# A float32 decoder trunk: 18 instead of 14 channel blocks of three FFN halves in Strassen pairs, with the products in another order

## The chip, the cores and the metric

The kernel runs on one core of one Trainium2 chip. The metric is the device time of one execution in microseconds, lower is better. The engines are named as the profile names them: PE (TensorE, matmul), PEld (its weight loads), DVE (VectorE), ACT (ScalarE), POOL (GpSimd) and SP (SyncE, which issues most DMAs).

## The reference, cut to what matters

Two layers work on x, 512 tokens by 1024 channels, all in float32. Each layer is an FFN half, a token mixer and a second FFN half, so there are four FFN halves. The change touches three of them.

```python
def swiglu(h, wg, wu, wd):
    return (jax.nn.silu(h @ wg) * (h @ wu)) @ wd

for li in range(DEPTH):                    # two layers
    h = rmsnorm(x, g[0])
    x = x + 0.5 * rmsnorm(swiglu(h, ffn_wg[li, 0], ffn_wu[li, 0], ffn_wd[li, 0]), g[1])
    ...                                    # the mixer of the layer
    h = rmsnorm(x, g[4])
    x = x + 0.5 * rmsnorm(swiglu(h, ffn_wg[li, 1], ffn_wu[li, 1], ffn_wd[li, 1]), g[5])
```

wg and wu are 1024 x 2816 and wd is 2816 x 1024. The 2816 hidden channels are 22 blocks of 128.

## The kernel before, in words

**Numbers.** Every float32 operand of a matmul is split into two float32r parts, hi and lo. A product takes three matmuls: hi by hi, hi by lo and lo by hi. The split of a weight block (128 x 1024) is an ACT copy to `whi` (L87) and a DVE subtraction to `wlo` (L88). h stands transposed in `self.hi` and `self.lo` (hT_hi, hT_lo in the trace): 8 chunks of 128 channels, 512 tokens each.

**Stages.** `PLAN` (L43) runs FFN (0,0), mixer 0, FFN (0,1), FFN (1,0), mixer 1, FFN (1,1). An FFN half (`ffn`, L691) has a lead of three blocks f = 0 to 2 (`lead`), then the rest of the 22 blocks, then the tail (`tail`, L549), which multiplies the 22 results g by wd into four accumulators `acc`, one for each 128 tokens, and runs the norms. FFN (0,0) uses plain blocks only and is not touched.

**A plain block** (L732 to L743) takes two weight blocks, wg and wu of one f. Each is 8 chunks by 3 matmuls of 512 columns (`chmajor`), 48 matmuls in all; then a Silu on ACT and a multiplication on DVE give g[f].

**A Strassen pair** (`paired_body`, L822) does two f at once, four weight blocks. Tokens are cut in halves and input channels in halves (quarters A11, A12, A21, A22 of h), output channels f and f+1 in columns of B11, B12, B21, B22. In the form of Winograd, seven products take the place of eight; each product is 2 (wg, wu) by 4 chunks by 3 = 24 matmuls of 256 columns. The left factors A11, A12, A22 are views of h; S1 to S4 are sums of quarters that `left_factors` (L759) makes once for each FFN half, on DVE through PSUM, and splits into SBUF tiles. S3 = A11 - A21 and S4 get small tiles of tag "g". The right factors T1 to T4 are sums of weight blocks, made on DVE in `prep_to` (L109, L112, L117, L120) ahead of their split. The seven products of a pair are, in the order of before: A11 into bank a, S2 into b, S1 into c, A12 added onto a, S3 added onto b, A22 into d, S4 added onto c. Between them ACT copies a (L858), and DVE makes the sums in the SBUF tile R: R1 = b + R0 (L861), R0 = b + R0 (L868), R2 = c + R0 (L869), R0 = d + R0 (L872), R1 = c + R1 (L876). So L869 has to read c after S3 and before S4 is added onto it. Silu and multiplication follow for each quarter (L865 to L879).

**Where the blocks stand.** f = 0 to 3 are plain (three of them the lead), f = 4 to 17 are seven pairs, and f = 18 to 21 are plain again, after the pairs. A21 is the one quarter of h that no product of a pair reads; the plain blocks read all of h.

**Buffers.** PSUM has four tiles of two banks (`bank2`), for the pairs a, b, c and d. Eight buffers each hold `whi` and `wlo` (`NW`): a split can run seven weight items ahead of PE. Four `raw` buffers (`NRAW`) take the loads of 512 KB; two buffers of tag "T" take T1 and T2/T4; 26 of tag "g" (`NG`) hold g, the parts of S3 and S4, and the splits of g for the tail.

**Order.** Inside `paired` and `tail` the order of PE is the one written. The order of the instructions on DVE, ACT and SP is chosen by the framework's planner, from its own estimate of times; each engine then takes its instructions in that order.

Of the kernel before, what the change touches and what calls it, by code (L numbers as in the profile page):

```python
# [33 lines left out]
AHEAD = {"mix0": 4, "mix1": 2}  # L34
LEAD = 3
NG = NF + 4
PAIRS = {("ffn", 0, 1): 7, ("ffn", 1, 0): 7, ("ffn", 1, 1): 7}
PLAIN = 4
SIDE = 6
SIDE_AT = 8  # L40
WARM = 20
# [8 lines left out]
class WeightStream:  # L50
# [18 lines left out]

    def add_pairs(self, fours):  # L70
        for four in fours:
            self.items += [(k, len(self.blocks)) for k in ("B11", "T2", "T1", "B21", "T3", "T4", "B22")]
            self.blocks += four

    def load_to(self, n):
# [15 lines left out]
    def prep_to(self, n):  # L91
        V, raw = self.nc.vector, self.raw
        while self.ready < min(n, len(self.items)):
            i = self.ready
            kind, r = self.items[i]
            self.ready += 1

            def t(k):
                raw[r, k] = self.t_pool.tile([P, 1024], F32, tag="T", name=f"T{k}_{r}", bufs=2)
                return raw[r, k]  # L100

            if kind == "block":
                self.load_to(r + 1)
                self.split(i, raw.pop(r))
                self.load_to(r + 1 + NRAW)
                continue
            self.load_to(r + {"B11": 2, "T2": 3, "T1": 3}.get(kind, 4))
            if kind == "B11":
                V.tensor_sub(t(1), raw[r + 1], raw[r])  # L109
                self.split(i, raw.pop(r))  # L110
            elif kind == "T2":
                V.tensor_sub(t(2), raw[r + 2], raw[r, 1])  # L112
                self.split(i, raw[r, 2])
            elif kind == "T1":
                self.split(i, raw.pop((r, 1)))
            elif kind == "B21":
                V.tensor_sub(raw[r, 2], raw[r + 3], raw[r, 2])  # L117
                self.split(i, raw.pop(r + 3))
            elif kind == "T3":
                V.tensor_sub(raw[r + 1], raw[r + 2], raw[r + 1])  # L120
                self.split(i, raw.pop(r + 1))
            elif kind == "T4":
                self.split(i, raw.pop((r, 2)))
            else:
                self.split(i, raw.pop(r + 2))
            self.load_to(r + {"B21": 5, "T3": 6, "T4": 6, "B22": 7}.get(kind, 4))

    def get(self, i, ahead=None):
        self.prep_to(i + 1 if ahead is None else ahead)
# [261 lines left out]
class Trunk:  # L391
# [24 lines left out]
    def phase_blocks(self, ph, ws):  # L416
        a = self.a
        if ph[0] == "ffn":
            _, li, s = ph
            n = PAIRS.get(ph, 0)  # L420

            def plain(fs):
                for f in fs:
                    ws.add([a["wg"][li, s, f], a["wu"][li, s, f]])

            plain(range(PLAIN))
            if n:
                ws.add_pairs([[a["gu"][li, s, e, k] for k in (0, 1, 3, 2)] for e in range(n)])
            plain(range(PLAIN + 2 * n, NF))
            return ws.add([a["wd"][li, s, f] for f in range(NF)])  # L430
        if ph[0] == "mix0":
            r = [a["even_in"][b, t] for b in (2, 1, 0) for t in range(4)]
            r += [a["even_out"][k] for k in range(4, 8)] + [a["glu"][t] for t in range(2)]
            return ws.add(r + [a["even_out"][k] for k in range(4)])
        if ph[0] == "mix1":
            q, f, cm, tm = 4, 8, a["odd_cm"], a["odd_tm"]
            r = [cm[i + h] for h in range(4) for i in (f, q)]
            r += [tm[b, t] for b in (1, 0, 2) for t in range(4)]
            return ws.add(r + [a["odd_out"][k] for k in range(KC)])
        raise ValueError(ph)  # L440
# [250 lines left out]
    def ffn(self, ph, nxt):  # L691
# [4 lines left out]
        with self.tc.tile_pool(name=f"ffn{nm}", bufs=1, reuse_waits="tile") as fp:  # L696
            self.room = fp
            g = {}
            side = None
            if ph == ("ffn", 0, 0):  # L700
                self.s5 = S5Tables(self, fp)
                side = self.s5.build()

            def gtile(dt, what):
                return fp.tile([P, S], dt, tag="g", name=f"{what}{nm}", bufs=NG)

            def act(f, pg):
                g[f] = gtile(F32, f"g{f}")
                nc.scalar.activation(g[f], pg[:, 0, :], AF.Silu)
                self.gated = nc.vector.tensor_mul(g[f], g[f], pg[:, 1, :]).ins  # L710

            split = {}

            def split_to(n):
                for e in range(n):
                    if e in g:
                        gh, gl = gtile(F32R, f"gh{e}"), gtile(F32R, f"gl{e}")
                        gv = g.pop(e)
                        nc.scalar.copy(gh, gv)
                        nc.vector.tensor_sub(gl, gv, gh.bitcast(F32))  # L720
                        split[e] = gh, gl

            n = PAIRS.get(ph, 0)
            ws.t_pool = fp
            self.lead(first, nm, act)
            if n:
                left = self.left_factors(gtile, fp, nm)
            if ph == PLAN[0]:
                self.masks(fp)
                with self.tc.issue_after(self.gated):  # L730
                    self.lower_bound()
            for f in (*range(LEAD, PLAIN), *range(PLAIN + 2 * n, NF)):  # L732
                if n and f == PLAIN + 2 * n:
                    self.paired(first + 2 * PLAIN, n, left, g, gtile, fp, nm)
                    left = None
                pg = self.bank2(f"gu{nm}_{f}")
                for j in range(2):
                    i = first + 2 * f + j + (3 * n if f >= PLAIN else 0)
                    last = self.chmajor(pg[:, j], ws.get(i, i + NW - 1))
                    ws.drop(i)  # L740
                if f == NF - 2:
                    split_to(2)
                act(f, pg)  # L743
                if side is not None:
                    self.s5.last, self.s5.chunk = last, f
                    for _ in range(NF if f == SIDE_AT + 7 else SIDE):
                        next(side, None)

            def stat(f):
                split_to(f + 2)  # L750
                return split.pop(f)

            self.g_post = self.load_gain(li, 2 * 2 * s + 1, "g_post")
            if nxt is not None:
                self.g_pre = self.load_gain(*self.pre_index(nxt), "g_pre")
            self.tail(NF, stat, first + 2 * NF + 3 * n, ph, nxt)
            self.room = None

    def left_factors(self, gtile, fp, nm):  # L759

# [47 lines left out]
        left["S4"] = done(s4, small("S4"))  # L810
        s3 = sums("S3")
        V.tensor_sub(s3, w11, w21)
        left["S3"] = done(s3, small("S3"))
        for name, q in (("A11", a11), ("A12", a12), ("A22", a22)):
            left[name] = tuple(views(v) for v in q)
        return left

    def paired(self, first, n, left, g, gtile, fp, nm):
        with self.tc.manual_schedule(engines={mybir.EngineType.PE}):
            self.paired_body(first, n, left, g, gtile, fp, nm)  # L820

    def paired_body(self, first, n, left, g, gtile, fp, nm):  # L822

# [20 lines left out]
        def new(name):  # L846
            return self.bank2(name)[:, :, 0:256]
# [1 line left out]
        state = {}  # L849

        for e in range(n):
            f = PLAIN + 2 * e
            R = fp.tile([P, 3, 512], F32, tag="R", name=f"R{nm}_{e}", bufs=2)
            R = R.rearrange("p a (m t) -> p a m t", m=2)
            g[f], g[f + 1] = gtile(F32, f"g{f}"), gtile(F32, f"g{f + 1}")
# [1 line left out]
            product(a, "A11", True, False)  # L857
            nc.scalar.copy(R[:, 0], a)  # L858
            b = new(f"sb{nm}_{e}")
            product(b, "S2", True, False)  # L860
            V.tensor_add(R[:, 1], b, R[:, 0])  # L861
            c = new(f"sc{nm}_{e}")
            product(c, "S1", True, False)
            product(a, "A12", False, True)
            nc.scalar.activation(g[f][:, 0:256], a[:, 0], AF.Silu)  # L865
            V.tensor_mul(g[f][:, 0:256], g[f][:, 0:256], a[:, 1])
            product(b, "S3", False, True)
            V.tensor_add(R[:, 0], b, R[:, 0])  # L868
            V.tensor_add(R[:, 2], c, R[:, 0])  # L869
            d = new(f"sd{nm}_{e}")  # L870
            product(d, "A22", True, True)
            V.tensor_add(R[:, 0], d, R[:, 0])  # L872
            nc.scalar.activation(g[f][:, 256:512], R[:, 0, 0], AF.Silu)
            V.tensor_mul(g[f][:, 256:512], g[f][:, 256:512], R[:, 0, 1])
            product(c, "S4", False, True)
# [643 lines left out]
def paired_blocks(wg, wu):  # L1519


    n = max(PAIRS.values())
    w = np.stack([wg, wu])[..., PLAIN * P:(PLAIN + 2 * n) * P].reshape(2, 2, 2, 2, 4, P, n, 2, P)
    return np.ascontiguousarray(w.transpose(1, 2, 6, 3, 7, 5, 0, 4, 8)).reshape(2, 2, n, 4, P, 1024)


# [37 lines left out]
```

## Time and profile before

| | us |
|---|---|
| median of 3 runs | 1933.02 (1931.67 to 1933.94) |
| the profiled execution | 1933.73 |
| its span, first to last instruction | 1932.0 |
| busy PE / DVE / ACT / POOL | 1854.2 / 1152.9 / 679.4 / 300.5 |

The busy time of PE overstates its work, since the ends of matmuls are modelled and overlap. The pace of PE is read from the starts of successive matmuls, and its gaps from the start of the last matmul of one product to the first of the next.

### The profile page before, as it was taken

The numbers are of one execution on the slowest core, as the hardware profiler recorded it, in microseconds if no ns is written. First come the engines' busy times: TensorE is split into PE (matmuls) and PEld (weight loads), VectorE is DVE, ScalarE is ACT, GpSimd is POOL, SyncE is SP. The second block draws the span as 40 slices with busy tenths as digits, with TensorE's granted clock in tenths as the row PEclk, the third lists the DMA queues.
The fourth block names the chain that finished last, engine by engine and source line by source line (L and its number), as shares of the span: only waits on it lengthen the run. The fifth ranks groups of instructions, "written<-read, shape, count | busy, mean of one in ns | idle before, by whom it ended". The sixth has DMA issues, their size and how long they took to land.

```text
span 1932.0 us, 26666 instructions
## 1 busy us (share of the span) xinstructions
PE 1854.2 (96%) x10760; PEld 1625.4 (84%) x10760; DVE 1152.9 (60%) x1739; ACT 679.4 (35%) x919; POOL 300.5 (16%) x530
## 2 busy tenths in 40 slices
PE   8999999989898999999999999999999989999998
PEld 8888888869787999888799998888988779998886
DVE  5756434285958887433698773428634598874333
ACT  4223323132243444332334442313434334443320
POOL 6037750032402000000100000003222020000000
PEclk8999999989999999999999999999999999999999
DMA  6434432243312333533213343332311123334311
GB/s 223 127 123 150 126 106 97 77 164 119 99 35 86 89 109 99 155 96 96 68 55 100 97 153 109 91 95 80 109 45 60 41 86 89 108 99 142 98 55 44
DMA packets 59595, 193.25 MB, mean 100 GB/s; under 512 B 6576, under 2 KB 13744, under 8 KB 59472
## 3 DMA queue, kind: packets, MB, share of 16 engines
q1 hardware_dynamic: 50544, 182.48, 30.4%
q10 hardware_dynamic: 7680, 5.24, 0.8%
q0 software_dynamic: 1248, 3.84, 0.6%
q8 instruction: 84, 1.38, 0.3%
q14 instruction: 39, 0.32, 0.0%
HBM read 182.10 MB, written 9.44 MB: 99 GB/s over the span
## 4 chain that ended last, share of the span: by engine, by line
PE 81%; DVE 12%; DMA 3%; ACT 2%; issue 2%; DVEq 0%; SPq 0%; ACTq 0%
PE accffn L647 16%; PE accffn L649 8%; PE guffn L547 7%; PE guffn L545 7%; PE guffn L546 7%; DMA raw<-in_gu_dram 3%; PE accmix L647 2%; PE scffn L840 2%; PE scffn L841 2%; DVE wlo L88 2%; PE scffn L842 2%; PE leadffn L546 2%; PE leadffn L545 2%; PE leadffn L547 2%; PE saffn L841 1%
## 5 line engine op out<-in xcount | busy, mean ns | idle before, releaser
L87 ACT CAST whi<-raw 128x1024 fp32r<-128x1024 f32 x314 | 328.7, 1050 | 701.2 <-PE accffn L649 183.5
L88 DVE TENSOR_TENSOR wlo<-raw,whi 128x1024 fp32r<-128x1024 f32 x270 | 332.3, 1231 | 406.8 <-ACT whi L87 406.4
L88 POOL TENSOR_TENSOR wlo<-raw,whi 128x1024 fp32r<-128x1024 f32 x44 | 106.8, 2453 | 1004.8 <-ACT whi L87 991.8
L545 PE MATMUL guffn<-hT_hi,whi 128*128 128x512 f32 x544 | 216.3, 398 | 0.0
L547 PE MATMUL guffn<-hT_hi,wlo 128*128 128x512 f32 x544 | 215.5, 396 | 0.0
L546 PE MATMUL guffn<-hT_lo,whi 128*128 128x512 f32 x544 | 213.8, 393 | 0.0
L547 PEld LDWEIGHTS guffn<-hT_hi,wlo 128*128 128x128 f32 x544 | 102.1, 188 | 25.0
L546 PEld LDWEIGHTS guffn<-hT_lo,whi 128*128 128x128 f32 x544 | 102.2, 188 | 24.5
L545 PEld LDWEIGHTS guffn<-hT_hi,whi 128*128 128x128 f32 x544 | 102.2, 188 | 23.5
L546 PE MATMUL leadffn<-hT_lo,whi 128*128 128x256 f32 x352 | 100.7, 287 | 0.0
L547 PE MATMUL leadffn<-hT_hi,wlo 128*128 128x256 f32 x352 | 100.7, 287 | 0.0
L545 PE MATMUL leadffn<-hT_hi,whi 128*128 128x256 f32 x352 | 100.5, 288 | 0.0
L842 PE MATMUL saffn<-hT_hi,wlo 128*128 128x256 f32 x336 | 94.9, 282 | 0.0
L841 PE MATMUL saffn<-hT_lo,whi 128*128 128x256 f32 x336 | 94.8, 282 | 0.0
L840 PE MATMUL saffn<-hT_hi,whi 128*128 128x256 f32 x336 | 94.4, 281 | 0.0
L87 ACT CAST whi<-T 128x1024 fp32r<-128x1024 f32 x63 | 66.3, 1052 | 72.8 <-issue 26.3
L88 DVE TENSOR_TENSOR wlo<-T,whi 128x1024 fp32r<-128x1024 f32 x63 | 76.8, 1218 | 9.2 <-ACT whi L87 9.2
L546 PEld LDWEIGHTS leadffn<-hT_lo,whi 128*128 128x128 f32 x352 | 68.1, 194 | 0.0
L545 PEld LDWEIGHTS leadffn<-hT_hi,whi 128*128 128x128 f32 x352 | 68.1, 195 | 0.0
L547 PEld LDWEIGHTS leadffn<-hT_hi,wlo 128*128 128x128 f32 x352 | 68.0, 193 | 0.0
L840 PEld LDWEIGHTS saffn<-hT_hi,whi 128*128 128x128 f32 x336 | 63.6, 189 | 0.1
L841 PEld LDWEIGHTS saffn<-hT_lo,whi 128*128 128x128 f32 x336 | 63.2, 188 | 0.1
(783 smaller groups left out, 4694.4 us busy)
## 6 DMA issues: line engine op xcount, KB each, us to landing
raw<-in_wd_dram SPq DMA_DIRECT2D x88, 512.0 KB, 3.6
raw<-in_gu_dram SPq DMA_DIRECT2D x84, 512.0 KB, 3.7
raw<-in_wg_dram SPq DMA_DIRECT2D x46, 512.0 KB, 3.7
raw<-in_wu_dram SPq DMA_DIRECT2D x46, 512.0 KB, 3.7
raw<-in_even_in_dram SPq DMA_DIRECT2D x12, 512.0 KB, 3.7
raw<-in_odd_tm_dram SPq DMA_DIRECT2D x12, 512.0 KB, 3.8
raw<-in_even_out_dram SPq DMA_DIRECT2D x8, 512.0 KB, 4.6
raw<-in_odd_cm_dram SPq DMA_DIRECT2D x8, 512.0 KB, 3.7
```

Of the source, the lines that this page charges most:

```text
L87: nc.scalar.copy(hi, raw)
L88: (nc.gpsimd if i in self.early else nc.vector).tensor_sub(lo, raw, hi.bitcast(F32))
L545: nc.tensor.matmul(out, sh, mh, start=start, stop=False)
L546: nc.tensor.matmul(out, sh, ml, start=False, stop=False)
L547: return nc.tensor.matmul(out, sl, mh, start=False, stop=stop).ins
L647: nc.tensor.matmul(acc[:, h, :], gh, w[:, h * 512:(h + 1) * 512], start=first, stop=False)
L649: nc.tensor.matmul(acc[:, h, :], gl, wh[:, h * 512:(h + 1) * 512], start=False, stop=stop)
L840: nc.tensor.matmul(o, wh[:, q], ah[k], start=start and k == 0, stop=False, skip_group_check=True)
L841: nc.tensor.matmul(o, wh[:, q], al[k], start=False, stop=False, skip_group_check=True)
L842: nc.tensor.matmul(o, wl[:, q], ah[k], start=False, stop=stop and k == 3, skip_group_check=True)
```

## The change

1. `PAIRS` goes from 7 to 9 for FFN (0,1), (1,0) and (1,1). f = 0 to 3 stay plain, f = 4 to 21 are nine pairs, and no plain block is left behind the pairs.
2. The factor S3 is no longer split into small tiles in `left_factors`. Its sum stays in PSUM until the plain block f = 3 is done; `rest()` then splits it into the place of the quarter A21 of hi and lo. So the tiles of tag "g" suffice for 22 g.
3. The order of the products is A11 into a, S2 into b, S1 into c, S3 into d, A12 onto a, A22 into b, S4 onto c. R0 is made as d + R1, and R2 = c + R0 follows it; both stand two products ahead of S4 instead of one. b is written anew by A22 instead of being added onto by S3.
4. In the weight stream T3 stands ahead of B21, with the loads moved to match.
5. The splits of g[0] and g[1] for the tail take the two buffers of tag "T" and are made in the last pair; before, they took tiles of tag "g" in the plain block f = 20.

```diff
-PAIRS = {("ffn", 0, 1): 7, ("ffn", 1, 0): 7, ("ffn", 1, 1): 7}
-PLAIN = 4
+PAIRS = {("ffn", 0, 1): 9, ("ffn", 1, 0): 9, ("ffn", 1, 1): 9}
...
-            self.items += [(k, len(self.blocks)) for k in ("B11", "T2", "T1", "B21", "T3", "T4", "B22")]
+            self.items += [(k, len(self.blocks)) for k in ("B11", "T2", "T1", "T3", "B21", "T4", "B22")]
...
-            self.load_to(r + {"B11": 2, "T2": 3, "T1": 3}.get(kind, 4))
+            self.load_to(r + {"B11": 2, "T2": 3, "T1": 3, "T3": 3}.get(kind, 4))
...
-            self.load_to(r + {"B21": 5, "T3": 6, "T4": 6, "B22": 7}.get(kind, 4))
+            self.load_to(r + {"T3": 5, "B21": 6, "T4": 6, "B22": 7}.get(kind, 4))
...
-            plain(range(PLAIN))
+            plain(range(NF - 2 * n))
             if n:
                 ws.add_pairs([[a["gu"][li, s, e, k] for k in (0, 1, 3, 2)] for e in range(n)])
-            plain(range(PLAIN + 2 * n, NF))
...
-                        gh, gl = gtile(F32R, f"gh{e}"), gtile(F32R, f"gl{e}")
+                        if ph in PAIRS and e < 2:
+                            t = fp.tile([P, 2, S], F32R, tag="T", name=f"gs{nm}_{e}", bufs=2)
+                            gh, gl = t[:, 0], t[:, 1]
+                        else:
+                            gh, gl = gtile(F32R, f"gh{e}"), gtile(F32R, f"gl{e}")
...
-            for f in (*range(LEAD, PLAIN), *range(PLAIN + 2 * n, NF)):
-                if n and f == PLAIN + 2 * n:
-                    self.paired(first + 2 * PLAIN, n, left, g, gtile, fp, nm)
-                    left = None
+            for f in range(LEAD, NF - 2 * n):
...
+            if n:
+                self.paired(first + 2 * (NF - 2 * n), n, left(), g, split_to, gtile, fp, nm)
...
         s3 = sums("S3")
         V.tensor_sub(s3, w11, w21)
-        left["S3"] = done(s3, small("S3"))
...
+        def rest():
+            left["S3"] = done(s3, [[v] for v in a21])
+            return left
+
+        return rest
...
             b = new(f"sb{nm}_{e}")
-            product(b, "S2", True, False)
+            product(b, "S2", True, True)
             V.tensor_add(R[:, 1], b, R[:, 0])
             c = new(f"sc{nm}_{e}")
             product(c, "S1", True, False)
+            d = new(f"sd{nm}_{e}")
+            product(d, "S3", True, True)
+            V.tensor_add(R[:, 0], d, R[:, 1])
+            V.tensor_add(R[:, 2], c, R[:, 0])
             product(a, "A12", False, True)
             nc.scalar.activation(g[f][:, 0:256], a[:, 0], AF.Silu)
             V.tensor_mul(g[f][:, 0:256], g[f][:, 0:256], a[:, 1])
-            product(b, "S3", False, True)
+            if e == n - 1:
+                split_to(2)
+            product(b, "A22", True, True)
             V.tensor_add(R[:, 0], b, R[:, 0])
-            V.tensor_add(R[:, 2], c, R[:, 0])
-            d = new(f"sd{nm}_{e}")
-            product(d, "A22", True, True)
-            V.tensor_add(R[:, 0], d, R[:, 0])
```

## Rows read from the trace of the kernel before

**Rows 1.** The page: span, chain that ended last, a costly group (busy, mean ns).

```profile
span 1932.0 us, 26666 instructions
...
PE 81%; DVE 12%; DMA 3%; ACT 2%; issue 2%; DVEq 0%; SPq 0%; ACTq 0%
...
L87 ACT CAST whi<-raw 128x1024 fp32r<-128x1024 f32 x314 | 328.7, 1050 | 701.2 <-PE accffn L649 183.5
```

**Rows 2.** Waits: who waited for whom, us in total, times, longest us.

```profile
PEld scffn L840 <- DVE Rffn L869: 19.9, 15, 1.8
PE scffn L840 <- DVE Rffn L869: 16.8, 15, 1.6
```

**Rows 3.** Windows: length, busy (count) PE, PEld, DVE, ACT, POOL; clock, DMA share, GB/s.

```profile
685.52:706.73 21.21, 20.24 (x171) 20.03 (x169) 17.16 (x20) 9.06 (x11) 0.00 (x0) 1.00 0.35 100
749.38:769.36 19.98, 19.98 (x171) 19.98 (x170) 15.41 (x18) 9.39 (x12) 0.00 (x0) 1.00 0.34 106
642.77:834.13 191.36, 186.09 (x1369) 176.29 (x1368) 127.51 (x142) 75.18 (x93) 0.00 (x0) 1.00 0.38 116
1015.25:1206.46 191.21, 186.10 (x1370) 176.30 (x1368) 127.98 (x142) 75.20 (x93) 0.00 (x0) 1.00 0.38 116
1608.01:1800.42 192.41, 186.02 (x1370) 176.22 (x1368) 127.47 (x142) 75.19 (x93) 0.00 (x0) 1.00 0.37 112
```

**Rows 4.** Timeline (start, us), PE: first matmuls of plain block f=21 and tail.

```profile
822.94 0.39 PE L545 MATMUL guffn<-hT_hi,whi 128*128 128x512 f32 x1
...
834.13 0.40 PE L647 MATMUL accffn<-whi,gh0ffn 128*128 128x512 f32 x1
```

**Rows 5.** Timeline, PE: first matmuls of A11, S3, A22, S4, next A11, third pair.

```profile
685.52 0.28 PE L840 MATMUL saffn<-hT_hi,whi 128*128 128x256 f32 x1
...
697.02 0.28 PE L840 MATMUL sbffn<-S3h0ffn,whi 128*128 128x256 f32 x1
...
699.82 0.28 PE L840 MATMUL sdffn<-hT_hi,whi 128*128 128x256 f32 x1
...
703.83 0.38 PE L840 MATMUL scffn<-S4h0ffn,whi 128*128 128x256 f32 x1 [0.97 <-DVE Rffn L869]
...
706.73 0.28 PE L840 MATMUL saffn<-hT_hi,whi 128*128 128x256 f32 x1
```

**Rows 6.** Timeline, PE: first matmuls of A11, S3, A22, S4, next A11, sixth pair.

```profile
749.38 0.28 PE L840 MATMUL saffn<-hT_hi,whi 128*128 128x256 f32 x1
...
760.88 0.28 PE L840 MATMUL sbffn<-S3h0ffn,whi 128*128 128x256 f32 x1
...
763.68 0.28 PE L840 MATMUL sdffn<-hT_hi,whi 128*128 128x256 f32 x1
...
766.56 0.28 PE L840 MATMUL scffn<-S4h0ffn,whi 128*128 128x256 f32 x1
...
769.36 0.28 PE L840 MATMUL saffn<-hT_hi,whi 128*128 128x256 f32 x1
```

**Rows 7.** Timeline, DVE, third pair, after its product S3.

```profile
700.21 1.23 DVE L109 TENSOR_TENSOR T<-raw,raw 128x1024 f32<-128x1024 f32 x1 [0.41 <-DMA raw<-in_gu_dram]
701.35 0.68 DVE L868 TENSOR_TENSOR Rffn<-sbffn,Rffn 128x512 f32<-128x512 f32 x1
701.95 1.22 DVE L88 TENSOR_TENSOR wlo<-T,whi 128x1024 fp32r<-128x1024 f32 x1
703.09 0.68 DVE L869 TENSOR_TENSOR Rffn<-scffn,Rffn 128x512 f32<-128x512 f32 x1
703.69 1.22 DVE L120 TENSOR_TENSOR raw<-raw,raw 128x1024 f32<-128x1024 f32 x1
704.82 1.22 DVE L112 TENSOR_TENSOR T<-raw,T 128x1024 f32<-128x1024 f32 x1
705.95 0.68 DVE L872 TENSOR_TENSOR Rffn<-sdffn,Rffn 128x512 f32<-128x512 f32 x1
```

**Rows 8.** Timeline, SP: load of a norm gain, queued among the weight loads.

```profile
775.30 0.39 SPq L488 DMA_DIRECT2D g_post<-in_norm_g_dram  x1
```

More of the change, by code (lines that the diff above doesn't have):

```diff
@@ L115, in prep_to @@
                 self.split(i, raw.pop((r, 1)))
+            elif kind == "T3":
+                V.tensor_sub(raw[r + 1], raw[r + 2], raw[r + 1])
+                self.split(i, raw.pop(r + 1))
             elif kind == "B21":
@@ L118, in prep_to @@
                 self.split(i, raw.pop(r + 3))
-            elif kind == "T3":
-                V.tensor_sub(raw[r + 1], raw[r + 2], raw[r + 1])
-                self.split(i, raw.pop(r + 1))
             elif kind == "T4":
@@ L731, in ffn @@
                     self.lower_bound()
-            for f in (*range(LEAD, PLAIN), *range(PLAIN + 2 * n, NF)):
-                if n and f == PLAIN + 2 * n:
-                    self.paired(first + 2 * PLAIN, n, left, g, gtile, fp, nm)
-                    left = None
+            for f in range(LEAD, NF - 2 * n):
                 pg = self.bank2(f"gu{nm}_{f}")
                 for j in range(2):
-                    i = first + 2 * f + j + (3 * n if f >= PLAIN else 0)
+                    i = first + 2 * f + j
                     last = self.chmajor(pg[:, j], ws.get(i, i + NW - 1))
@@ L812, in left_factors, with paired, paired_body @@
         V.tensor_sub(s3, w11, w21)
-        left["S3"] = done(s3, small("S3"))
         for name, q in (("A11", a11), ("A12", a12), ("A22", a22)):
             left[name] = tuple(views(v) for v in q)
-        return left
-    def paired(self, first, n, left, g, gtile, fp, nm):
+        def rest():
+            left["S3"] = done(s3, [[v] for v in a21])
+            return left
+        return rest
+    def paired(self, first, n, left, g, split_to, gtile, fp, nm):
         with self.tc.manual_schedule(engines={mybir.EngineType.PE}):
-            self.paired_body(first, n, left, g, gtile, fp, nm)
-    def paired_body(self, first, n, left, g, gtile, fp, nm):
+            self.paired_body(first, n, left, g, split_to, gtile, fp, nm)
+    def paired_body(self, first, n, left, g, split_to, gtile, fp, nm):
         nc, ws = self.nc, self.ws
@@ L851, in paired_body @@
         for e in range(n):
-            f = PLAIN + 2 * e
+            f = NF - 2 * n + 2 * e
             R = fp.tile([P, 3, 512], F32, tag="R", name=f"R{nm}_{e}", bufs=2)
@@ L1522, in paired_blocks @@
     n = max(PAIRS.values())
-    w = np.stack([wg, wu])[..., PLAIN * P:(PLAIN + 2 * n) * P].reshape(2, 2, 2, 2, 4, P, n, 2, P)
+    w = np.stack([wg, wu])[..., -2 * n * P:].reshape(2, 2, 2, 2, 4, P, n, 2, P)
     return np.ascontiguousarray(w.transpose(1, 2, 6, 3, 7, 5, 0, 4, 8)).reshape(2, 2, n, 4, P, 1024)
```

## The prediction

> **What bounds the kernel now.** I read the page first. PE carries 81% of the chain that ended last and DVE 12%; the span is 1932.0 us, and the execution took 1933.73, so 1.73 lie around the span [rows 1]. A chain that is PE for four fifths says that matmul time comes off the end one for one, and the DVE share says that PE also waits for DVE somewhere. So I asked next who waited for whom. The first matmul of S4 waits for L869, the sum R2 = c + R0, 15 times, on the weight-load side and on the matmul side alike; the two rows are the same 15 waits seen by both halves of the engine and are not to be added [rows 2]. There are 21 pairs (7 in each of 3 FFN halves), so 15 of them stall.
>
> Then the prices, from starts of matmuls, since their ends are modelled. The clock in the stages concerned is 1.00 of 2.4 GHz throughout, so the clock plays no part [rows 3]. A plain block runs from 822.94 to 834.13: 11.19 us [rows 4]. A pair without the stall, the sixth, runs from 749.38 to 769.36: 19.98 us. In it the four products ahead of S3 take 11.50 (2.88 each, rounded), S3 2.80, A22 2.88, S4 2.80 [rows 6]. So products on the small tiles of S3 and S4 are 0.08 us shorter than those on views of h. A stalled pair, the third, takes 21.21: A22 starts at 699.82 and S4 only at 703.83, 4.01 later where 2.88 would do [rows 5]. Two plain blocks cost 22.38, so a stalled pair wins only 1.17 over them and a free one 2.40.
>
> The stall itself is read on DVE. S3 ends about 699.82, where A22 starts. DVE is then idle at the head of its queue for a DMA, makes L109 for a later pair (700.21), then L868 (701.35), then a weight split (701.95), and only then L869 (703.09 to 703.77), 0.06 ahead of S4 [rows 5, 7]. The lag from the end of S3 to the end of L869 is 3.95 us, and one product, 2.88, is all the cover it has. The longest of the 15 waits is 1.8 [rows 2], a lag near 4.7.
>
> **The sum over the three stages.** From the first pair to the tail the stages take 191.36, 191.21 and 192.41, 574.98 together [rows 3]. As a test of the prices: 7 x 19.98 + 4 x 11.19 = 184.62 each, 553.86 together; the other 21.1 us are the stalls, 1.4 in each of 15. After the change each stage is nine pairs.
> - *The two blocks swapped for a pair*, six times: 22.38 - 19.98 = 2.40 each, 14.4 us gained.
> - *The order of the products.* R0 and R2 now follow S3 with A12 and A22 between them and S4: cover 5.75 instead of 2.88. A lag of 3.95 to 4.7 fits with 1.0 us to spare, so I take the whole 21.1 as gained. The other end is nothing gained (below).
> - *S3 in the place of A21.* Its matmuls then read a view of h like A11's: 2.88 instead of 2.80, 0.08 x 27 = 2.2 us lost. The end on the other side is 0, if the short pace is not tied to the tile; I take the loss, since both products on small tiles in rows 6 have 2.80 and all on views have 2.88.
>
> A pair becomes 20.06, a stage 180.5, the three 541.6: 33.4 us less.
>
> **What I cost at nothing, and its cover.**
> - *The late split of S3.* It can start only when f = 3 has ended, where the first pair begins: one ACT copy of 128x1024 (1.05 us [rows 1]) and one DVE subtraction (about 1.2, as the 128x1024 rows of [rows 7]). S3 is needed 3 products later, at 8.63; what may queue ahead on DVE (two or three operations of 1.13) still fits. Its PSUM tile stays taken until then; A11 and S2 have other tiles and S1 starts 5.75 in. If A11 had to wait for it, it would be 2.3 us, 6.8 for three stages: the other end. Below nothing it can't go, as f = 3 has no PE gap to give back.
> - *The tail's start.* The third accumulator may take c's bank: L876 has to read it after the last S4. Two accumulators of six matmuls of 0.233 (11.19 / 48 [rows 4]) go first, 2.80 us; L876 takes 0.7 and at most one split of 1.2 ahead of it. Cover enough; with a second split 0.5 us, 1.6 in three tails. Before, plain blocks stood here.
> - *g[0], g[1] split in the last pair*: two short ACT copies and DVE subtractions, where no sums for a next pair are left to make. The tag-T buffers that they wait for were read one pair earlier.
> - *More weight sums.* Six more pairs mean 24 more sums and 18 more splits on DVE. DVE is busy 17.16 in a stalled pair, ACT 9.06 [rows 3]: 86% and 45% of 20.06.
> - *Loads.* Four of 512 KB in 20.06 instead of 21.21; the DMA share of 0.35 [rows 3] becomes 0.37. T3 ahead of B21 frees one raw buffer as early as B21 did. The two norm gains wait on SP for S2's last product [rows 8], now late in the last pair; behind them stand loads of wd blocks needed at least three products later.
>
> For these edges I add 0.8 us in all, an estimate between 0 and the 8.4 of the ends, and nearer to 0: the stage sum above, of pairs, plain blocks and stalls, leaves no room for a gap at either edge now [rows 3].
>
> Profiled execution: 1933.73 - 33.4 + 0.8 = 1901.1. That execution lies 0.7 above the median of the runs, so the median forecast is 1900.4, taken as 1900.5.
>
> **The rivals.**
> *DVE is the clock.* The free pairs are the last two of each stage, for which no further sums are made: DVE is busy 15.41 there against 17.16 [rows 3]. So no row shows a pair with the full load at 20 us. If the stall is only where DVE's lateness comes out, it comes out elsewhere and 21 pairs (7 of 9, as 5 of 7 now) keep 1.4 us: 29.4 lost again, 1930. The Trainium skill speaks for this one: "Trainium Kernel Development and Optimization", Best Practices, warns that tiling speeds up the matmuls but not the evacuation of PSUM, and a Strassen pair trades just so. Against it: 17.16 is 2.9 below 20.06, and the idle time of DVE in the row is spent waiting on others. Chance 0.10, of which 0.04 within 0.2%.
>
> *The wait moves to b, lightly.* b is now read last by the sum after A22, and the next pair's S2 writes it anew: cover S4 and A11, 5.68. Before, that sum (L872) read d, which was not needed for six products. Its lag is now 706.63 - 702.70 = 3.9 [rows 5, 7], behind L120 and L112. Each further 128x1024 operation that the planner puts ahead costs 1.13. With two more the lag is 6.2: 0.5 in 21 pairs, 11 us, 1911. Chance 0.10.
>
> *The same, heavily: slower than before.* Three more operations and one wait of 0.41 for a load at the head of DVE's queue [rows 7] make a lag of 7.7, 2.05 in each of 21 pairs, 43 us: 1943. It decides from 1.77 a pair, a lag near 7.45. For it speaks that the planner does place sums for later pairs ahead of urgent ones (L109 ahead of L868); against it, that the number of operations between is the same as before and their places are released by the same products. Chance 0.08.
>
> **How the numbers follow.** The forecast, 1900.5, has 0.72. Its own bounds: 1897.5 without the loss on S3, 1906 with most of the edges at their dear end; other stages are planned anew too, and equal stages differ by 1.2 us already [rows 3], so 1895 to 1906. To hold 8 in 10 the range takes in the light wait on b: 1895 to 1913. A measurement of this kernel tells 0.2%, 3.9 us, from no change. Faster: 0.72 + 0.10 + 0.06 = 0.88; same 0.04; slower 0.08.
>
> **What would show it.** Right: no row of waits in which S4's first matmul waits for the R2 sum; pairs 20.06 apart from the second to the eighth; S3 at 2.88; stages near 180.5 and the tail starting with no gap. Wrong: a first matmul of A11 or S2 waiting for DVE (b or a not yet read); A11 of the first pair waiting for the split of S3; DVE busy to the brim in the pairs; pairs that stay at 21.

## The result, and the profile after

| | us |
|---|---|
| before, median of 4 runs beside it | 1933.48 (1931.67 to 1935.71) |
| after, median of 4 runs | 1900.69 (1899.38 to 1902.05) |
| ratio | 0.983, 95% interval 0.9813 to 0.9847 |
| the profiled execution of after | 1899.38 |

The forecast was 1900.5, from 1895 to 1913. The page of after, span and chain, against [rows 1]:

```profile
span 1897.6 us, 27701 instructions
...
PE 89%; DVE 8%; issue 1%; ACT 1%; DMA 0%; DVEq 0%; SPq 0%; ACTq 0%
```

PE's share of the chain went from 81% to 89%, DVE's from 12% to 8%. The windows, against [rows 3] (columns as there): the third pair, then the three stages from the first pair to the tail.

```profile
681.12:701.19 20.07, 20.07 (x171) 20.07 (x170) 17.19 (x20) 8.98 (x11) 0.00 (x0) 1.00 0.35 105
640.99:821.58 180.59, 180.59 (x1513) 180.59 (x1512) 149.51 (x166) 81.81 (x101) 0.00 (x0) 1.00 0.40 120
1002.72:1183.32 180.60, 180.60 (x1514) 180.59 (x1512) 149.31 (x166) 81.82 (x101) 0.00 (x0) 1.00 0.39 120
1585.39:1765.99 180.60, 180.60 (x1513) 180.60 (x1512) 149.21 (x166) 81.86 (x101) 0.00 (x0) 1.00 0.38 117
```

In each of the four, PE is busy for the whole length. The stages add up to 541.79 against 574.98, so 33.2 us of the gain lie in them; the span fell by 34.4. The waits of after have no row for S4's first matmul. In its place stands a row of the opposite sense, DVE waiting for the product S3 (us in total, times, longest us):

```profile
DVE Rffn L873 <- PE sdffn L849: 15.4, 24, 0.7
```

The timeline of PE in after (start, us): S3, A12, S4 and the next A11 in the third pair, then the last matmul of the ninth pair and the first of the tail.

```profile
689.75 0.28 PE L847 MATMUL sdffn<-hT_hi,whi 128*128 128x256 f32 x1
...
692.63 0.28 PE L847 MATMUL saffn<-hT_hi,whi 128*128 128x256 f32 x1
...
698.39 0.28 PE L847 MATMUL scffn<-S4h0ffn,whi 128*128 128x256 f32 x1
...
701.19 0.28 PE L847 MATMUL saffn<-hT_hi,whi 128*128 128x256 f32 x1
...
821.47 0.28 PE L849 MATMUL scffn<-S4h1ffn,wlo 128*128 128x256 f32 x1
821.58 0.64 PE L645 MATMUL accffn<-whi,gsffn 128*128 128x512 f32 x2
```

S3 takes 2.88 (689.75 to 692.63), S4 2.80 (698.39 to 701.19), and the tail follows the last pair at the pace of the matmuls. The timeline of DVE in the same pair, which answers to [rows 7]:

```profile
692.83 0.69 DVE L873 TENSOR_TENSOR Rffn<-sdffn,Rffn 128x512 f32<-128x512 f32 x1 [0.63 <-PE sdffn L849]
693.55 0.69 DVE L874 TENSOR_TENSOR Rffn<-scffn,Rffn 128x512 f32<-128x512 f32 x1
694.16 1.22 DVE L87 TENSOR_TENSOR wlo<-raw,whi 128x1024 fp32r<-128x1024 f32 x1
696.02 1.23 DVE L108 TENSOR_TENSOR T<-raw,raw 128x1024 f32<-128x1024 f32 x1 [0.64 <-DMA raw<-in_gu_dram]
697.16 1.22 DVE L87 TENSOR_TENSOR wlo<-T,whi 128x1024 fp32r<-128x1024 f32 x1
698.29 0.42 DVE L877 TENSOR_TENSOR g8ffn<-g8ffn,saffn 128x256 f32<-128x256 f32 x1
698.63 0.68 DVE L881 TENSOR_TENSOR Rffn<-sbffn,Rffn 128x512 f32<-128x512 f32 x1
```

R0 (L873) and R2 (L874) now follow S3 at once: R2 ends at 694.24, 1.6 after S3's end at 692.63, and 4.15 before S4. The sum T1 (L108), the one that waits for a load at the head of DVE's queue, stood ahead of them in [rows 7] (there L109); here it stands behind. Its place in the pair hardly moved: 14.69 us after the pair's start before (685.52 to 700.21), 14.90 after (681.12 to 696.02). S3's end moved, from 14.30 into the pair to 11.51. Between the first pair and the tail, T1 is made five times in a stage of seven pairs and seven times in a stage of nine, each time two pairs ahead of its use (an experiment below shows it). The 15 stalls of [rows 2] are one for each of these T1; the last two pairs of a stage, which make none, run free.

### The profile page after: what moved, and what is told of

It is laid out like the page before. It is cut to its first block, busy times and chain, and to the rows that moved or that the text cites. A ratio compares the mean times of both kernels' runs of the same rounds, so it can differ in the third digit from the quotient of the medians.

```text
span 1897.6 us, 27701 instructions
## 1 busy us (share of the span) xinstructions
PE 1837.0 (97%) x11192; PEld 1638.0 (86%) x11192; DVE 1220.2 (64%) x1814; ACT 701.1 (37%) x946; POOL 302.0 (16%) x530
## 4 chain that ended last, share of the span: by engine, by line
PE 89%; DVE 8%; issue 1%; ACT 1%; DMA 0%; DVEq 0%; SPq 0%; ACTq 0%
PE accffn L645 16%; PE accffn L647 8%; PE guffn L543 4%; PE guffn L545 4%; PE guffn L544 4%; PE saffn L848 3%; PE sbffn L848 3%; PE sbffn L847 3%; PE sbffn L849 3%; PE saffn L849 3%; PE saffn L847 3%; PE scffn L848 3%; PE scffn L849 3%; PE scffn L847 3%; PE accmix L645 2%; PE leadffn L544 2%
## 5 line engine op out<-in xcount | busy, mean ns | idle before, releaser
L543 PE MATMUL guffn<-hT_hi,whi 128*128 128x512 f32 x352 | 141.0, 401 | 0.0
L545 PE MATMUL guffn<-hT_hi,wlo 128*128 128x512 f32 x352 | 138.8, 394 | 0.0
L544 PE MATMUL guffn<-hT_lo,whi 128*128 128x512 f32 x352 | 138.1, 392 | 0.0
L848 PE MATMUL saffn<-hT_lo,whi 128*128 128x256 f32 x432 | 122.1, 283 | 0.0
L849 PE MATMUL saffn<-hT_hi,wlo 128*128 128x256 f32 x432 | 122.0, 282 | 0.0
L847 PE MATMUL saffn<-hT_hi,whi 128*128 128x256 f32 x432 | 121.2, 281 | 0.0
L849 PEld LDWEIGHTS saffn<-hT_hi,wlo 128*128 128x128 f32 x432 | 81.2, 188 | 0.0
L545 PEld LDWEIGHTS guffn<-hT_hi,wlo 128*128 128x128 f32 x352 | 66.1, 188 | 17.0
L544 PEld LDWEIGHTS guffn<-hT_lo,whi 128*128 128x128 f32 x352 | 66.1, 188 | 15.3
L543 PEld LDWEIGHTS guffn<-hT_hi,whi 128*128 128x128 f32 x352 | 66.1, 188 | 15.0
```

What stands on the lines that cost most here:

```text
L543: nc.tensor.matmul(out, sh, mh, start=start, stop=False)
L544: nc.tensor.matmul(out, sh, ml, start=False, stop=False)
L545: return nc.tensor.matmul(out, sl, mh, start=False, stop=stop).ins
L847: nc.tensor.matmul(o, wh[:, q], ah[k], start=start and k == 0, stop=False, skip_group_check=True)
L848: nc.tensor.matmul(o, wh[:, q], al[k], start=False, stop=False, skip_group_check=True)
L849: nc.tensor.matmul(o, wl[:, q], ah[k], start=False, stop=stop and k == 3, skip_group_check=True)
```

## The experiments

Two theories of why the stall went. *Distance*: two products of cover where one was too little, as the prediction has it. *DVE*: the engine is short of time, and the stall is only where that shows; then the gain should be given back when DVE gets more work. A third came later: *T1*, the order on DVE alone. Ratios are to runs of the kernel before on the same chip.

**Seven pairs, the new order.** `PAIRS` 9 to 7. By the changed loop the plain blocks f = 3 to 7 come first and all seven pairs behind them, where before the last four plain blocks stood behind the pairs.

> The changed kernel with seven pairs in place of nine: f = 0 to 7 plain, then seven pairs in the new order, S3 in the place of A21. It tells the order of the products from the number of pairs. Theory (the two gains are apart, 21 us by the order and 14 us by the two more pairs): a stage is 7 x 20.06 + 4 x 11.19 = 185.2 us, the three 555.6, 13.8 more than the changed kernel has; time about 1914.5, no wait of S4 for the sum R2. Rival (the order did nothing, the stalls went because no plain blocks and their loads stand behind the pairs): five of seven pairs stall by 1.4 us and the time is near 1935.

1908.08 (1907.72 to 1910.36), ratio 0.9864 (0.9849 to 0.9879). The windows of its first stage of pairs, and of the lead ahead of it:

```profile
684.38:824.84 140.46, 140.46 (x1177) 140.45 (x1176) 114.55 (x127) 63.83 (x79) 0.00 (x0) 1.00 0.39 121
590.76:628.38 37.62, 36.51 (x305) 36.30 (x304) 31.72 (x40) 14.67 (x18) 5.19 (x3) 1.00 0.29 88
```

140.46 is seven times 20.07: the new order ends every stall with seven pairs too. The rival is not settled by this run, since here too no plain block stands behind the pairs; the next run settles it. But this run is 6 us faster than expected. The lead takes 37.62 here and, in after,

```profile
590.39:629.71 39.32, 36.78 (x305) 36.28 (x304) 35.02 (x44) 14.68 (x17) 5.16 (x3) 1.00 0.20 67
```

1.70 longer, with 3.3 more of DVE; in the other two halves 1.46 and 2.00, so 5.2 in all. The six swapped pairs are worth 6 x (22.38 - 20.07) = 13.9; less 5.2 that is 8.7, and the two spans differ by 8.6 (1906.2 and 1897.6). DVE's timeline in that lead of after shows what stands in the way, three sums for the first pair ahead of the norm (L519) of the last tokens, and PE waiting for that norm:

```profile
601.26 1.22 DVE L108 TENSOR_TENSOR T<-raw,raw 128x1024 f32<-128x1024 f32 x1
...
603.59 1.21 DVE L111 TENSOR_TENSOR T<-raw,T 128x1024 f32<-128x1024 f32 x1
604.73 1.22 DVE L116 TENSOR_TENSOR raw<-raw,raw 128x1024 f32<-128x1024 f32 x1
...
607.13 1.28 DVE L519 SCALAR_TENSOR_TENSOR xnmix<-x,y2mix_0b,g_pre 128x1024 f32<-128x1024 f32 x1
...
608.57 1.06 PE L534 MATMUL ptmix<-ident,xnmix 128*128 128x128 f32 x8 [1.44 <-DVE xnmix L519]
```

With plain blocks between lead and pairs those sums come later. The kernel before, with its pairs right behind f = 3 too, pays the same: its lead takes 39.1 (592.37 to 631.48).

**Nine pairs, the old order.** The order of products and weights of before; S3 still in A21's place.

```diff
-            product(b, "S2", True, True)
+            product(b, "S2", True, False)
...
-            d = new(f"sd{nm}_{e}")
-            product(d, "S3", True, True)
-            V.tensor_add(R[:, 0], d, R[:, 1])
-            V.tensor_add(R[:, 2], c, R[:, 0])
             product(a, "A12", False, True)
...
+            product(b, "S3", False, True)
+            V.tensor_add(R[:, 0], b, R[:, 0])
+            V.tensor_add(R[:, 2], c, R[:, 0])
...
```

> The changed kernel with the old order of products (A11, S2, S1, A12, S3 added onto b, A22 into d, S4) and the old weight order, but nine pairs, S3 in the place of A21 and no plain block behind. Theory (the cover of one product is what stalls): seven of nine pairs in each stage stall by 1.4 us, 29 us in all, time near 1930, and the wait of S4's first matmul for the sum R2 is back, about 21 times. Rival (the order is not the cause): time near 1901 and no such wait.

1927.51 (1925.39 to 1928.8), ratio 0.9963 (0.9949 to 0.9976). The waits of this run:

```profile
PE scffn L847 <- DVE Rffn L876: 21.0, 21, 1.4
```

Seven stalls in each stage of nine, though no plain block stands behind the pairs. So the nine pairs alone win 6.3 us, with six more stalls than before, and the order some 26 on top.

**One product of cover, S3 in its own bank.** A12 back ahead of S3, with the old order of T3 and B21; everything else as in after.

```diff
...
+            product(a, "A12", False, True)
+            nc.scalar.activation(g[f][:, 0:256], a[:, 0], AF.Silu)
+            V.tensor_mul(g[f][:, 0:256], g[f][:, 0:256], a[:, 1])
             d = new(f"sd{nm}_{e}")
             product(d, "S3", True, True)
...
```

> The changed kernel with S3 moved behind A12: A11, S2, S1, A12, S3 into its own bank d, A22 into b, S4. So the sums R0 and R2 have one product between them and S4, as before the change, but S3 is not added onto b. It tells the distance from the bank. Theory (distance): the stall is back as in the old order, 1.4 us in some 21 pairs, time near 1930. Rival (the reuse of bank b was what held the sums up): time near 1901.

1927.91 (1926.39 to 1928.89), ratio 0.9963 (0.995 to 0.9975), 21 waits again. The bank and the form of R0 are not the cause. DVE's timeline in a stalled pair that starts at 707.82, with S3 ending at 722.20:

```profile
722.62 1.23 DVE L108 TENSOR_TENSOR T<-raw,raw 128x1024 f32<-128x1024 f32 x1 [0.52 <-DMA raw<-in_gu_dram]
723.76 0.68 DVE L876 TENSOR_TENSOR Rffn<-sdffn,Rffn 128x512 f32<-128x512 f32 x1
724.36 1.21 DVE L87 TENSOR_TENSOR wlo<-T,whi 128x1024 fp32r<-128x1024 f32 x1
725.50 0.68 DVE L877 TENSOR_TENSOR Rffn<-scffn,Rffn 128x512 f32<-128x512 f32 x1
```

This is [rows 7] over again, and T1 stands at 14.80 into the pair. It left two readings that I had taken for one: the cover is too short, or T1 is in front.

**T1 behind the sums.** The kernel of the last run, with T1 for the next pair issued behind R2 of this one, which takes it out of the place above; the weight items behind the next B11 are prepared only after that. The same cover of one product.

```diff
...
             if kind == "B11":
-                V.tensor_sub(t(1), raw[r + 1], raw[r])
-                self.split(i, raw.pop(r))
+                if r not in self.later:
+                    V.tensor_sub(t(1), raw[r + 1], raw[r])
+                self.split(i, raw[r])
             elif kind == "T2":
+                if r in self.later:
+                    with self.tc.issue_after(self.r2):
+                        V.tensor_sub(t(1), raw[r + 1], raw[r])
+                raw.pop(r)
...
```

> The order with one product between S3 and S4, as in the run that put A12 ahead of S3, with one thing more: the sum T1 for the next pair is put behind R2 of this one. Same results, same work. The traces show T1 start 14.7 to 14.9 us into a pair in the kernel before, in the changed one and in that run, right after its load has landed; S3 ends 14.3 to 14.4 into the pair where A12 stands ahead of it and 11.5 where it does not. Theory of the distance: one product, 2.88 us, is too little cover, the 21 waits of S4 stay, about 1928. Theory of T1: the sums are late only because T1 waits for its load at the head of DVE's queue ahead of them; with T1 behind them R0 and R2 end some 1.6 us after S3, under the 2.88 of cover, no wait of S4 is left, pairs are 20.07 and the time is about 1901 (up to 1906 if T1, some 1 us later, makes another wait).

1900.94 (1899.64 to 1901.61), ratio 0.9829 (0.9812 to 0.9845): as fast as after. In place of the 21 waits of S4 there is one, in the last pair of the first stage, which makes no T1; weight splits stand ahead of R0 and R2 there:

```profile
PE scffn L857 <- DVE Rffn L888: 0.5, 1, 0.5
```

The third pair's window and DVE's timeline in it:

```profile
681.42:701.49 20.07, 20.07 (x171) 20.07 (x169) 17.12 (x20) 8.66 (x12) 0.00 (x0) 1.00 0.36 105
```

```profile
696.01 0.69 DVE L887 TENSOR_TENSOR Rffn<-sdffn,Rffn 128x512 f32<-128x512 f32 x1 [2.04 <-PE sdffn L859]
696.73 0.69 DVE L888 TENSOR_TENSOR Rffn<-scffn,Rffn 128x512 f32<-128x512 f32 x1
697.34 1.22 DVE L117 TENSOR_TENSOR T<-raw,raw 128x1024 f32<-128x1024 f32 x1
```

S3 ends at 695.81, R2 at 697.42, S4 starts at 698.69: with nothing in front, a lag of 1.6 fits under one product with 1.3 to spare. So the stall was T1 with its wait for the load, ahead of R0, and the split between R0 and R2; this run takes both out of the way and doesn't part them. By the rows of the stalled pair above either alone might do, an estimate: without the split R2 ends 2.84 after S3, without T1 and its wait about 2.6, against 2.88 of cover. The order of T3 and B21 is the old one here, so that part of the change isn't what ends the stall either. Moving S3 ahead, as the change does, ends it too, since R0 and R2 are then done before T1's load has landed; that the longer cover would do it by itself isn't shown.

**The sums behind T1.** After, with R0 of each pair but the last issued behind the T1 for the next pair, to see whether two products cover the old lag.

```diff
-                V.tensor_sub(t(1), raw[r + 1], raw[r])
+                self.t1 = V.tensor_sub(t(1), raw[r + 1], raw[r]).ins
...
-            V.tensor_add(R[:, 0], d, R[:, 1])
+            if e < n - 1:
+                with self.tc.issue_after(ws.t1):
+                    V.tensor_add(R[:, 0], d, R[:, 1])
+            else:
+                V.tensor_add(R[:, 0], d, R[:, 1])
```

> The changed kernel with R0 (and so R2) of a pair put behind the sum T1 for the next pair, in the 24 pairs that have a next one. Same results, same work, two products between S3 and S4 as in the changed kernel. Theory of the distance: the sums take a lag of 3.95 to 4.7 behind S3 as before, within the cover of 5.75, no wait, about 1901. Theory of T1: T1 runs from 14.9 to 16.0 us into the pair, R0 ends near 16.7, and with a weight split between them as before R2 ends near 18.5, while S4 could start at 17.27: 1.2 to 1.4 lost in 21 to 24 pairs, 25 to 34 us, 1926 to 1934; with no split between only 0.1 to 0.3 a pair, about 1905.

1900.61 (1900.23 to 1903.75), ratio 0.9832 (0.9817 to 0.9847). The edit missed. DVE in the third pair:

```profile
693.75 0.69 DVE L876 TENSOR_TENSOR Rffn<-sdffn,Rffn 128x512 f32<-128x512 f32 x1 [0.63 <-PE sdffn L850]
...
696.87 1.23 DVE L108 TENSOR_TENSOR T<-raw,raw 128x1024 f32<-128x1024 f32 x1 [0.58 <-DMA raw<-in_gu_dram]
```

R0 is still ahead of the T1 of this place. So that T1 is the one for the pair after the next, and the one I named had been made a pair earlier. Whether two products would have covered sums that stand behind T1 was not tried: T1 would end near 16.1 into the pair and S4 starts at 17.27, which leaves 1.2 for two sums of 0.7; by these rows, hardly.

**More work for DVE.** From the third pair on, T1 is made three times, and in a second kernel five times; the extra sums have the same result and change nothing else.

```diff
                 V.tensor_sub(t(1), raw[r + 1], raw[r])
+                for _ in range(2 if r in self.more else 0):
+                    V.tensor_sub(raw[r, 1], raw[r + 1], raw[r])
```

> The changed kernel with the sum T1 of the third to ninth pair of each stage made three times over, so two more DVE operations of 128x1024 in 21 pairs, 2.27 us of DVE each. It tests whether DVE is the clock. Theory (PE is the clock, DVE has 20.06 - 17.19 = 2.9 us to spare in a pair): DVE is busy 19.5 of 20.06 us, the time is 1901 to 1906. Rival (DVE is the clock already): 21 x 2.27 = 48 us more, 1948.

1900.24 (1899.04 to 1901.94), ratio 0.9822 (0.9806 to 0.9837): no change, with this third pair:

```profile
683.82:703.88 20.06, 20.06 (x170) 20.06 (x169) 19.10 (x22) 9.19 (x11) 0.00 (x0) 1.00 0.36 105
```

> As e4_two_more_sums, but with T1 made five times over: four more DVE operations of 128x1024 in 21 pairs, 4.54 us of DVE each. Theory (PE is the clock up to 20.06 us of DVE in a pair, DVE beyond): 17.2 + 4.5 = 21.7 us of DVE in a pair, so at least 1.7 more in each of 21 pairs, 35 us or a little over, time near 1936. Rival (something else bounds the pairs, and DVE has more room than its busy time says): time below 1915.

1930.56 (1928.7 to 1932.14), ratio 0.999 (0.998 to 1.0). All of the gain is gone, but not evenly. Windows: the third pair, then a product S2 of the seventh and the product behind it:

```profile
683.74:703.80 20.06, 20.06 (x170) 20.06 (x169) 19.47 (x22) 8.56 (x10) 0.00 (x0) 1.00 0.26 74
...
769.50:775.62 6.12, 5.45 (x24) 5.16 (x25) 6.12 (x7) 5.40 (x6) 0.00 (x0) 0.52 0.14 22
775.62:778.92 3.30, 3.30 (x25) 3.30 (x25) 3.30 (x4) 0.33 (x1) 0.00 (x0) 0.85 0.86 298
```

The first five pairs keep 20.06; splits run up to seven weight items ahead, and I take it that this stock is used up first. Then PE waits, not for R2 but for the weights:

```profile
769.50 0.38 PE L852 MATMUL sbffn<-hg_postffn,whi 128*128 128x256 f32 x1 [1.86 <-ACT whi L89]
```

and the granted clock drops to 0.52 for that product. So DVE is not the bound at 17.19 of 20.07, nor with two more sums; with four more it is.

**S3 and S4 change places.** S3 in small tiles and S4 in the place of A21.

```diff
-        left["S4"] = done(s4, small("S4"))
         s3 = sums("S3")
         V.tensor_sub(s3, w11, w21)
+        left["S3"] = done(s3, small("S3"))
...
-            left["S3"] = done(s3, [[v] for v in a21])
+            left["S4"] = done(s4, [[v] for v in a21])
```

> The changed kernel with the places of S3 and S4 exchanged: S3 in the small tiles of tag g, S4 split late into the place of A21. It tells whether the pace of a product is tied to the place of its left factor. Theory (it is): the product S3 takes 2.80 us, S4 2.88, the time stays at 1901 within 2. Rival (the pace is tied to the product's place in the sequence): S3 stays at 2.88 and S4 at 2.80.

1903.11 in one execution. PE's timeline, S4 to the next A11, then S3 of that pair to its A12:

```profile
681.36 0.29 PE L847 MATMUL scffn<-hT_hi,whi 128*128 128x256 f32 x1
...
684.24 0.29 PE L847 MATMUL saffn<-hT_hi,whi 128*128 128x256 f32 x1
...
692.88 0.28 PE L847 MATMUL sdffn<-S3h0ffn,whi 128*128 128x256 f32 x1
...
695.71 0.28 PE L847 MATMUL saffn<-hT_hi,whi 128*128 128x256 f32 x1
```

S4 takes 2.88 and S3 2.83, in a pair of 20.10. The pace follows the place more than the factor, though 2.83 is not quite 2.80.

**All tiles moved by 64 bytes.** A tile of 64 bytes for each partition ahead of all others.

```diff
+        pad = self.cp.tile([P, 16], F32, tag="pad", name="pad")
+        nc.vector.memset(pad, 0.0)
```

> The changed kernel with all SBUF tiles moved up by 64 bytes in each partition, nothing else. It tells whether the two paces of a product (2.88 us on views of h and on S1 and S2, 2.80 on the small tiles) go by the address of the left factor. If they do, products change their pace, S4 from 2.80 to 2.88 or those on h from 2.88 to 2.80 (2.1 us of the time for each product that changes in 27 pairs). If not, all seven keep theirs and the time stays within 2 us of 1901.

1899.51 in one execution, and the seven products keep their paces (S4 2.80, the others 2.87 to 2.88). What makes the short pace stays open.

**Three attempts on what is left.** First, the T sums of the first pair held back behind the last transposed part of h, to take them out of the norm's way:

```diff
-                V.tensor_sub(t(1), raw[r + 1], raw[r])
+                with self.tc.issue_after(self.turned):
+                    V.tensor_sub(t(1), raw[r + 1], raw[r])
```

and T2 and T3 likewise.

> The changed kernel with the sums T1, T2 and T3 held back on DVE behind the last turn of h in the lead. In e1_seven_pairs each lead was 1.5 to 2.0 us shorter, and its DVE rows had no such sums inside the chain of the norm. Theory (three sums, 3.4 us of DVE, stand in the way of the norm chain of the last 128 tokens, on which PE waits): each of the three leads is 1.5 to 2.0 us shorter, 5 us in all, time near 1896. Rival (DVE is full through the lead and f = 3, so the sums come late for the first pair instead): the gain comes back as a wait in the first pair, time 1899 to 1903.

1909.64 (1907.09 to 1909.7), ratio 0.9879 (0.9863 to 0.9895): slower than after by 9. The sums now stand ahead of the left factors, which free a PSUM tile for f = 3, and the first matmul of f = 3 waits for that in each of the three stages:

```profile
PE guffn L547 <- DVE S4ffn L815: 8.3, 3, 2.8
```

Without this wait the first and third lead are 1.5 and 1.9 us shorter than in after; the second is not (45.1 against 45.0). The wait also costs more than its 8.3 us. The windows of f = 3, in the three stages of this run and, last, in the first stage of after:

```profile
631.24:645.26 14.02, 14.02 (x48) 11.16 (x49) 10.99 (x11) 3.20 (x4) 0.00 (x0) 0.78 0.19 63
998.73:1011.55 12.82, 12.82 (x49) 10.23 (x49) 10.90 (x11) 3.13 (x4) 0.00 (x0) 0.87 0.23 74
1583.11:1595.78 12.67, 12.67 (x49) 10.15 (x49) 10.99 (x11) 3.13 (x4) 0.00 (x0) 0.88 0.15 45
...
629.71:640.99 11.28, 11.28 (x49) 9.09 (x49) 11.28 (x12) 4.79 (x6) 0.00 (x0) 1.00 0.23 55
```

Behind the wait the granted clock is 0.78 to 0.88, and f = 3 takes 5.7 us longer in the three stages together.

Second, the same sums behind the first operation of S4 in `left_factors`, and no weight item of a pair prepared in the lead:

```diff
-            self.lead(first, nm, act)
+            self.lead(first, nm, act, cap=first + 2 * (NF - 2 * n))
...
-        V.tensor_sub(s4, a12[0].bitcast(F32), s2)
+        self.ws.hold = V.tensor_sub(s4, a12[0].bitcast(F32), s2).ins
...
-                V.tensor_sub(t(1), raw[r + 1], raw[r])
+                with self.tc.issue_after(self.hold):
+                    V.tensor_sub(t(1), raw[r + 1], raw[r])
```

> As e7_sums_held_back, but the sums of weight blocks stand on DVE behind the first operation of S4 in the left factors, not only behind the last turn of h; in e7 three of them came ahead of S1 and S2, and the block f = 3 then waited 2.8 us for the PSUM tile that S2 gives back. Theory (left factors first, sums later, DVE has the time since the first pair needs T2 only 2.9 us in): each lead is 1.5 to 2.0 us shorter and f = 3 starts without a wait, 4 to 5 us in all, time near 1896. Rival (DVE is full from the last turn to the first pair, so whatever is put last is late): a wait of 1 to 3 us at T2 or T1 of the first pair of each stage, time 1900 to 1908.

1896.4 (1894.86 to 1897.42, 5 runs), ratio 0.9814 (0.98 to 0.9827): the fastest here, 4.3 under after's median, and its five runs all lie below after's four. Each against the kernel before beside it, the gains are 35.8 and 32.8, and the intervals of the two ratios overlap, so by the times alone the gain over after is small and not certain. The trace shows it, for the two edits together. Its first lead takes 37.34 (39.32 in after), the others 43.50 and 45.79 (45.00 and 47.80), 5.5 us less in all; S4's operation comes first and the first T sum right behind it:

```profile
623.70 1.22 DVE L815 TENSOR_TENSOR S4ffn<-hT_hi,S2ffn 128x1024 f32<-128x1024 f32 x1
624.83 1.22 DVE L109 TENSOR_TENSOR T<-raw,raw 128x1024 f32<-128x1024 f32 x1
```

Third, three pairs in FFN (0,0) as well, f = 16 to 21, with the left factors made during f = 15.

```diff
-PAIRS = {("ffn", 0, 1): 9, ("ffn", 1, 0): 9, ("ffn", 1, 1): 9}
+PAIRS = {("ffn", 0, 0): 3, ("ffn", 0, 1): 9, ("ffn", 1, 0): 9, ("ffn", 1, 1): 9}
...
             for f in range(LEAD, NF - 2 * n):
+                if ph == PLAN[0] and f == 15:
+                    left = self.left_factors(gtile, fp, nm)
```

> The changed kernel with three pairs also in FFN (0,0), for its blocks f = 16 to 21; its left factors are made during f = 15, beside the end of the tables of mixer 0. Theory (a pair is worth 22.38 - 20.06 = 2.32 us wherever PE is the clock): 7.0 us less, time near 1894. Rival (DVE can't make left factors and the first sums in the one block of 11.2 us, some 14 us of DVE work): a wait of 3 to 8 us ahead of the first of the three pairs, time 1897 to 1902.

1916.35 (1912.47 to 1917.97), ratio 0.9915 (0.99 to 0.993): slower than after by 15.7. Two new waits, one in front of f = 15 and one in the tail of this FFN half, cost more than the 3 x 2.31 that the pairs could win:

```profile
PE guffn L543 <- DVE g14ffn L708: 8.8, 1, 8.8
...
PE accffn L645 <- ACT gh2ffn L721: 4.6, 1, 4.6
```

As in the run with the sums held back, more is lost behind the waits. The block f = 15 takes 13.98 in place of 11.2, at a granted clock of 0.79. The tail is 8.6 longer (123.43 against 114.79, to its first transpose), 5.6 of it waits. The lead of this half is 3.2 longer as well (42.95 against 39.72), for a cause that was not looked for.

## Why the prediction was right, and where it was not

- *The swap and the price of a pair.* Right: a pair of 20.07 against 20.06 forecast, stages of 180.6 against 180.5, together 33.2 shorter against 33.4. Sizes read from starts of matmuls of one unstalled pair [rows 6] carried over to 27. That the median came within 0.2 of the forecast is chance: the profiled execution came out 1.7 below its forecast (1899.38 against 1901.1), but it also lies 1.3 under the median of its runs, where the prediction had counted the one of before 0.7 over.
- *The stalls, 21.1 us.* The size was right, the reason only half. I gave the cover as 5.75 against an unchanged lag of 3.95 to 4.7, with 1.0 to spare. The lag itself fell to 1.6, and 4.15 is spare, because S3 ends 3.4 us before the load of T1 lands instead of 0.4. With T1 and the split out of the way one product of cover does it (1900.94). I had T1 in [rows 7] and counted it as part of a lag that would travel with S3; it starts when its load lands, at 14.6 to 14.9 into the pair in before, in after and in the run with a cover of one. Both ways of counting give no stall, so the time alone could not tell them apart.
- *S3 at 2.88.* Right, 0.08 x 27 lost. The prediction left the other end open, "if the short pace is not tied to the tile"; with the factors swapped the pace moved with the tile (2.83 and 2.88).
- *The late split of S3.* Wrong, and to my favour: "it can start only when f = 3 has ended". ACT's timeline in after has it ahead of the first pair at 640.99, released by a matmul of f = 3:

```profile
638.44 1.02 ACT L795 CAST hT_hi<-S3ffn 128x1024 fp32r<-128x1024 f32 x1 [0.25 <-PE guffn L545]
```

  It needs the last read of A21's quarter, not of the whole block: A21 is the first four of the eight chunks, and the copy starts 2.55 us before the block ends, about as long as the 12 matmuls of the other four take (2.80).
- *The tail and the edges.* The tail starts with no gap, and 0.8 for the edges was not needed. The span came out 1.2 lower outside the stages; the first pair starts 1.8 earlier (640.99 against 642.77), in a part that the change does not touch but the planner plans anew.
- *DVE is the clock.* Fell: nine pairs in a row at 20.07 and none late, with DVE busy 17.19 in the third, and 19.10 cost nothing. The sentence of the Trainium skill behind it ("Trainium Kernel Development and Optimization", Best Practices), that tiling speeds up the matmuls and not the evacuation of PSUM, doesn't bite at this load. How near DVE is to being the bound the run with four more sums shows (1930.56): between two and four sums a pair. Those sums read weight blocks in SBUF, so no run here tests the evacuation of PSUM by itself.
- *The wait moves to b.* Fell, light and heavy: b's sum L881 ends at 699.31, 0.9 after A22's end where I had 3.9, since two T sums stood ahead of it in [rows 7] and stand behind it here. The next S2 comes 4.8 later.

What I saw nowhere beforehand is the cost in the leads, 5.2 us, older than the change: a loss that the waits list in small rows of PE (one, for `xnffn`, mixed with a longer wait elsewhere), not as one.

## What to carry to other kernels

When an urgent operation is late on a shared engine, look at what stands ahead of it and what that in turn waits for; if it is a transfer's landing, its time need not move with the producer. Here it ended the stall to move the producer to the other side of the landing, and also to hold the one instruction back; a longer cover by itself was not tried. Price a repeated unit from the start-to-start time of one that is not stalled, and test the sum against the stages of the trace before using it. Work that an engine's spare time and the stock of prepared operands absorb shows nothing at first (five pairs, in the run with four more sums), so test the reserve by adding work rather than by reading busy shares. When an edit makes PE wait, look at the granted clock behind the wait too.

## What the hardware showed that I had not expected

- The same 24 matmuls of 256 columns take 2.80 or 2.88 us by the place of the moving operand (2.83 for S3 in the small tiles). Moving every tile by 64 bytes left both paces as they were; the cause is open.
- A wait of PE cost more than its own length. With four more sums, a gap of 1.86 us on PE was followed by a product S2 at a granted clock of 0.52, near the lower of the two levels (1.2 GHz), which took 6.12 us in place of 2.87, a second wait of 0.67 in it. With the sums held back, a gap of 2.78 was followed by f = 3 at 0.78, which took 14.02 in place of 11.28.
- With four more sums the three stages grew by 30.6 us up to the end of their last S4 (in two of them 1.4 us of the tail's matmuls stand ahead of it and are not counted). The list of waits has 11.0 of it (S2's first matmuls for ACT) and 5.9 (for `wlo` on DVE). The other 13.7 were not parted; lost clock is among them.
